# Bias strips read backwards from overlapping table rows, and x copied out of PSUM once

## The chip, the cores and the metric

The kernel runs on one core of a Trainium2 chip. The metric is the device time of one execution in microseconds (us). Three runs of the kernel before took 2470.0, 2471.08 and 2473.52 us; their median is 2471.08 us.

## The reference

Two layers of a decoder trunk over one sequence of 512 tokens with 1024 channels, all in float32. Each layer does the following.

```python
h = rms_norm(x, g)                       # per token: x * rsqrt(mean(x*x) + eps) * g
proj = h @ w_in                          # one projection, cut into q, k, v, gates of two mixers
y_ret = (silu(g_r) * retention(q_r, k_r, v_r)) @ w_o_ret
y_nsa = nsa(q_n, kv_n, gate_n, ..., rel_bias) @ w_o_nsa
x = x + (sigmoid(m_a) * y_ret + sigmoid(m_b) * y_nsa) @ w_out
x = x + swiglu(rms_norm(x, g_ffn))       # feed-forward with 2816 hidden channels
```

`nsa` has 16 heads and three branches per head: compressed keys (31 blocks), selected blocks and a window. With 512 tokens the selected blocks and the window are both plain causal attention. Every softmax adds a bias that depends on the head and on the distance between query and key alone: `rel_bias[bucket(q - k), head]`. Distances below 16 have a bucket each, longer ones share buckets by their logarithm, and all from 128 on share the last. Keys ahead of the query are masked.

## The kernel before

**Layout and precision.** Activations are kept transposed, eight tiles of 128 channels by 512 tokens. Every float32 operand of a product is split into a rounded part `hi` and a rest `lo`: ScalarE (ACT) writes `hi` with a copy, VectorE (DVE) writes `lo` as the difference (`split`, L78; `split_scaled`, L82, which also multiplies by a gain per channel). A product is then three matmuls, hi·hi, hi·lo and lo·hi (`mm3`, L119). Weights come through the SP queue in pieces of up to 1 MB into three buffers `wr` (`raw`, L86) and are split into tiles `wh` and `wl`, three of each (`cut`, L94).

**Order of the work.** The Python code names the order in which instructions are issued to a planner. The planner sorts the instructions of each engine when the kernel is built, by what it takes to be ready, and hands out the buffers of one tag one after the other in program order. On the chip each engine works through its own list in that order, and so do the queues of SP, ACT and POOL (GpSimd), which issue the DMAs. Most small tiles share the tag `u` with 37 buffers.

**The stretch before the first attention head.** `setup` (L133) loads x in eight tiles (SP), gains (SP), the identity and masks (POOL), and transposes the gains into `cols` (L163, L165). `setup_bias` (L187) makes the bias of every head against distance with a small one-hot product (L196) and writes it to a DRAM table `bv` of 16 rows with 640 entries: 384 entries of the far value, then 256 entries of near distances in falling order (L198 to L201). `near_strips` (L203) reads from `bv` one tile per pair of heads in which partition p holds the row from entry p on (L211, POOL queue). Such a tile has the tokens in the wrong order, so it is multiplied by an anti-diagonal matrix `anti` (L216), copied out (L218) and written to a second DRAM table `nr` (L220, ACT queue). The products stand where `nsa_kv` runs the generator to its end (L322).

`start_x` (L265) transposes x on TensorE (PE), tile k into one PSUM bank. From that bank ACT writes `hh` (the gain times x, rounded), DVE writes `hl` (the rest), and ACT copies x itself into `xt` (L281), which the ACT queue stores to DRAM (L282). DVE also sums the squares of x (L274). The norm's factor per token is not in `h`; it is applied after the projections. It is worked out by `norm_stats` (L244, POOL does the power, L253) and spread over a tile `rb` by `norm_bcast` (L255: DVE writes `rep`, PE transposes it at L262, ACT copies it out at L263).

`nsa_kv` (L294) projects compressed keys and values (bank `f`, weights `wc`), then two key tiles (bank `a`, weights `wk`). `compress` (L352) multiplies by `rb`, adds position vectors (L366, L377), splits, and runs a product over 16 rows (L391). Then come queries and values.

**The attention heads.** `nsa` (L657) runs 16 heads in a pipeline over 18 steps. Each head has a strip of 128 x 512 biases (`bias_strip`, L223: two loads, the far half from `bv`, broadcast, and the near half from `nr`; eight buffers). `nsa_scores` (L517) takes the last (i+1)·128 columns of it in one DVE instruction that subtracts, adds the bias and takes the minimum (L537), and `nsa_cmp` (L466) reads every sixteenth column (L489). Other projections fill PE between the heads. Behind the heads come the retention, the mixing and the feed-forward part, and the second layer goes the same way.

Of the kernel before, what the change touches and what calls it, by code (L numbers as in the profile page):

```python
# [8 lines left out]
F32 = mybir.dt.float32  # L9
F32R = mybir.dt.float32r  # L10
AF = mybir.ActivationFunctionType
ALU = mybir.AluOpType
AX = mybir.AxisListType

P = 128
T = 512
D = 1024
NT = T // P
KD = D // P
# [3 lines left out]
HN = 16  # L23
# [4 lines left out]
BIG = 3e38  # L28
# [3 lines left out]
class Builder:  # L32
# [47 lines left out]
        (eng or self.nc.vector).tensor_sub(lo, src, hi.bitcast(F32))  # L80

    def split_scaled(self, hi, lo, src, col):  # L82
        self.nc.scalar.activation(hi, src, AF.Copy, scale=col)  # L83
        self.nc.vector.scalar_tensor_tensor(lo, src, col, hi.bitcast(F32), ALU.mult, ALU.subtract)  # L84

    def raw(self, srcs, kt, n):  # L86
# [46 lines left out]
    def setup(self):  # L133
        nc, a = self.nc, self.a
        self.bv = self.dr.tile([HN, 640], F32, tag="bv", name="bv")
        self.nr = self.dr.tile([HN, P, 256], F32, tag="nr", name="nr")
        self.ident = self.const("ident", [P, P])
        nc.gpsimd.dma_start(self.ident, a["c_ident"])
        rows = self.u("rows", w=P)

        def load_rows():
            for l in range(DEPTH):
                nc.sync.dma_start(rows[l * 8 : l * 8 + 8], a["norm_mix_g"][l].rearrange("(k p) -> k p", p=P))
                nc.sync.dma_start(rows[16 + l * 8 : 24 + l * 8], a["norm_ffn_g"][l].rearrange("(k p) -> k p", p=P))
            nc.sync.dma_start(rows[32:40], a["norm_final_g"].rearrange("(k p) -> k p", p=P))
            nc.sync.dma_start(rows[40:72], a["cmp_pos_k"].rearrange("l (r q) d -> (l r) (q d)", q=2))
            nc.sync.dma_start(rows[72:104], a["cmp_pos_v"].rearrange("l (r q) d -> (l r) (q d)", q=2))

        self.xnat = []
        for hf in range(2):  # L150
            for t in range(NT):
                xt = self.u("xnat")
                nc.sync.dma_start(xt, a["x"][0, t * P : (t + 1) * P, hf * 512 : (hf + 1) * 512])
                self.xnat.append(xt)
            if hf == 0:
                load_rows()
        self.setup_bias()
        self.anti = self.sb.tile([P, P], F32, tag="u", name="anti")
        nc.gpsimd.dma_start(self.anti, a["c_anti"])
        self.strips = self.near_strips()  # L160
        next(self.strips)
        ps = self.tp()
        nc.tensor.transpose(ps[:, :104], rows[:104, :], self.ident[:104, :104])  # L163
        self.cols = self.const("cols", [P, 104])
        nc.vector.tensor_copy(self.cols, ps[:, :104])  # L165
        self.gmix = [self.cols[:, l * 8 : l * 8 + 8] for l in range(DEPTH)]
        self.gffn = [self.cols[:, 16 + l * 8 : 24 + l * 8] for l in range(DEPTH)]
        self.pos = {"k": [self.cols[:, 40 + l * 16 : 56 + l * 16] for l in range(DEPTH)],
                    "v": [self.cols[:, 72 + l * 16 : 88 + l * 16] for l in range(DEPTH)]}
        self.mhalf = self.const("mhalf", [P, NT])  # L170
        nc.vector.memset(self.mhalf, -0.5)
        self.ones = self.const("ones", [P, 1])
        nc.vector.memset(self.ones, 1.0)
        self.rb = self.const("rb", [P, T])
        self.rstd = self.const("rstd", [P, NT])
        self.hrstd = self.const("hrstd", [P, NT])
        self.kcz = [self.const(f"kcz{g}", [P, 224], F32R) for g in range(2)]
        for g in range(2):
            nc.vector.memset(self.kcz[g].bitcast(F32), 0.0)
        self.xs = self.dr.tile([KD, P, T], F32, tag="xs", name="xs")  # L180
        self.gs = self.dr.tile([2 * KD, P, T], F32, tag="gs", name="gs")
        self.gr = self.dr.tile([4 * NSPILL, P, T], F32, tag="gr", name="gr")
        self.ys = self.dr.tile([KD, P, T], F32, tag="ys", name="ys")
        self.cmask = self.const("cmask", [P, NT, 32])
        nc.gpsimd.dma_start(self.cmask, a["c_cmask"].rearrange("p (i n) -> p i n", n=32))

    def setup_bias(self):  # L187

        nc, a = self.nc, self.a
        tab = self.u("tab", w=HN)  # L190
        nc.scalar.dma_start(tab[:32], a["rel_bias"])
        nc.vector.memset(tab[32:33], NEG)
        ohv = self.u("ohv", w=256)
        nc.scalar.dma_start(ohv[:33], a["c_ohv"])
        ps = self.mm()
        nc.tensor.matmul(ps[:HN, :256], tab[:33], ohv[:33], start=True, stop=True)  # L196
        near, far = self.u("near", w=256), self.u("far", w=384)
        nc.scalar.activation(near[:HN], ps[:HN, :256], AF.Copy)  # L198
        nc.vector.tensor_copy(far[:HN], ps[:HN, 0:1].broadcast_to([HN, 384]))
        nc.gpsimd.dma_start(self.bv[:, :384], far[:HN])  # L200
        nc.gpsimd.dma_start(self.bv[:, 384:], near[:HN])  # L201

    def near_strips(self):  # L203


        nc = self.nc
        back = []
        for t in range(HN // 2):
            b = self.u("back").rearrange("p (b n) -> p b n", b=2)
            row = self.bv[t : t + 1, 256 : 512]  # L210
            nc.gpsimd.dma_start(b, bass.AP(row.tensor, row.offset, [[1, P], [8 * 640, 2], [1, 256]]))  # L211
            back.append(b)
        yield
        for t in range(HN // 2):
            ps = self.tp()
            nc.tensor.matmul(ps, self.anti, back[t].rearrange("p b n -> p (b n)"), start=True, stop=True)  # L216
            near = self.u("near").rearrange("p (b n) -> p b n", b=2)
            nc.scalar.activation(near, ps.rearrange("p (b n) -> p b n", b=2), AF.Copy)  # L218
            for b in range(2):
                nc.scalar.dma_start(self.nr[t + 8 * b], near[:, b])  # L220
            yield

    def bias_strip(self, h):  # L223

        t = self.sb.tile([P, T], F32, tag="strip", name=self.nm("strip"), bufs=NST)
        self.nc.sync.dma_start(t[:, :256], self.bv[h : h + 1, :256].broadcast_to([P, 256]))
        self.nc.sync.dma_start(t[:, 256:], self.nr[h])
        return t


    def make_h(self, src, col):
# [12 lines left out]
    def norm_stats(self, acc=None, ss=None):  # L244
        nc = self.nc
        if ss is None:
            ps = self.tp()
            for t in range(NT):
                nc.tensor.matmul(ps[:, t : t + 1], acc[:, t * P : (t + 1) * P], self.ones, start=True, stop=True)
            ss = ps[:, :NT]  # L250
        var = self.small("var", NT)
        nc.vector.tensor_scalar(var, ss, 1.0 / D, 1e-6, ALU.mult, ALU.add)
        nc.gpsimd.tensor_tensor(self.rstd, var, self.mhalf, ALU.pow)  # L253

    def norm_bcast(self):  # L255
        nc = self.nc
# [8 lines left out]
    def start_x(self):  # L265
# [3 lines left out]
        for k in range(KD):  # L269
# [6 lines left out]
            for t in range(NT):  # L276
                nc.tensor.transpose(ps[:, t * P : (t + 1) * P], self.xnat[4 * (k // 4) + t][:, (k % 4) * P : (k % 4 + 1) * P],
                                    self.ident)
            h.append(self.make_h(ps, self.gmix[0][:, k : k + 1]))
            xt = self.u("xt")  # L280
            nc.scalar.activation(xt, ps, AF.Copy)  # L281
            nc.scalar.dma_start(self.xs[k], xt)  # L282

        def stats():
            s2 = self.small("s2", NT)
# [8 lines left out]
    def nsa_kv(self, l, h, q0):  # L294
        nc, w = self.nc, self.a["w_in"][l]
        view = lambda c, n, k0=0, kt=KD: w[k0 * P : (k0 + kt) * P, c : c + n].rearrange("(k p) n -> p k n", p=P)
        wc = self.wcols(w, 0, KD, C_KV, 256)
        psc = [self.proj_t(wc, j, h, "f") for j in range(2)]
        wk = self.raw([(lambda v: v[:, :, :P], view(C_KV + 256, P)), (lambda v: v[:, :, P:], view(C_KV + 512, P))], KD, 256)
        self.stats()  # L300
# [18 lines left out]
            next(comp[kind])  # L319
        psk.append(self.proj_t([self.cut(wk[:, :, P:])], 0, h, "a"))  # L320
        keys(0)
        for _ in self.strips:  # L322
            pass
        next(comp["k"])
        for _ in range(2):
            for _ in range(9):
# [139 lines left out]
    def nsa_cmp(self, quad, qs, heads, pc):  # L466
# [16 lines left out]
        nc.gpsimd.memset(z, NEG)  # L483
        for i in range(NT):
            n = min(NCMP, 7 + 8 * i)
            x0 = 415 - P * i
            for s in range(4):
                bias = heads[4 * quad + s]["strip"][:, x0 : x0 + 16 * (n - 1) + 1 : 16]
                nc.vector.tensor_tensor(z4[:, i, s, :n], p4[:, i, s, :n], bias, ALU.add)  # L489
            yield  # L490
        z3 = z.rearrange("p (c n) -> p c n", n=32)
# [25 lines left out]
    def nsa_scores(self, st):  # L517
# [15 lines left out]
        def soft(br, i, src):  # L533
            w = (i + 1) * P
            p = pr[br][i]
            c = slice(br * NT + i, br * NT + i + 1)
            nc.vector.tensor_tensor_reduce(p, src, strip[:, T - w :], -1.0, BIG, ALU.add, ALU.min, nmx[:, c])  # L537
            nc.scalar.activation(p, p, AF.Exp, scale=-1.0, bias=nmx[:, c], accum_out=sm[:, c])  # L538

        for i in range(2):  # L540
# [466 lines left out]
def constants():  # L1007
# [14 lines left out]
    dec = np.where(e >= 0, gam[:, None, None] ** np.maximum(e, 0) / 16.0, 0.0).astype(f)  # L1022
    return {
        "c_ident": np.eye(P, dtype=f),
        "c_anti": np.ascontiguousarray(np.eye(P, dtype=f)[::-1]),
        "c_cos": np.ascontiguousarray(np.cos(ang).T.astype(f)),
        "c_sin": np.ascontiguousarray(np.sin(ang).T.astype(f)),
        "c_ohv": onehot(511 - np.arange(384, 640)),
        "c_cmask": cmask,
        "c_dec": dec,  # L1030
    }
# [28 lines left out]
```

## Time and profile before

| | |
|---|---|
| median of three runs | 2471.08 us |
| the profiled execution, its own time | 2472.11 us |
| its span, first to last instruction | 2470.1 us |
| PE busy | 2410.7 us, 98% |
| DVE busy | 1408.9 us, 57% |
| ACT busy | 1031.1 us, 42% |
| POOL busy | 252.9 us, 10% |
| mean granted TensorE clock | 0.996 |

The profile is of one execution. A line of the timeline has the start in us, the duration, the engine, the line of the code, the tile written and the tiles read, how many instructions were merged, and in brackets the idle time before it with what ended it. PE's matmuls overlap in their pipeline, so their cost on a busy PE is the distance from one start to the next and not the duration shown. The engines SPq, ACTq and POOLq stand for the queues that issue DMAs.

### The profile page before, as it was taken

How to read it: one execution, taken by the hardware profiler on the slowest of the kernel's cores; microseconds unless marked ns; L12 is line 12 of the kernel's file. 1: busy time of each engine (PE TensorE's matmuls, PEld its weight loads, DVE VectorE, ACT ScalarE, POOL GpSimd, SP SyncE). 2: the span in 40 equal slices, each digit the busy share in tenths (PEclk: the TensorE clock that was granted, in tenths of full speed). 3: DMA queues.
4: the chain of work that ended last, by engine and by line, in shares of the span. 5: the costliest groups of instructions: out<-in, count | busy, mean ns of one | idle time of the engine just before them, and what ended most of it. 6: DMA issues, size and time to landing. Idle time of an engine off the chain costs nothing.

```text
span 2470.1 us, 29520 instructions
## 1 busy us (share of the span) xinstructions
PE 2410.7 (98%) x11131; PEld 1956.7 (79%) x11131; DVE 1408.9 (57%) x2796; ACT 1031.1 (42%) x1871; POOL 252.9 (10%) x226
## 2 busy tenths in 40 slices
PE   6999999999999999999989999999999999999998
PEld 4887778788888778888878777878888878888887
DVE  5678887444655643333467888864545655433334
ACT  4666666233333432222346666642333333322223
POOL 2000000010111121010110000001100301101010
PEclk9999999999999999999999999999999999999999
DMA  7632223523334422323345332235223424223221
GB/s 222 190 94 77 73 86 78 175 80 100 107 99 145 145 94 85 103 87 101 114 139 146 90 82 69 73 90 171 89 91 105 158 96 147 92 85 98 90 94 60
DMA packets 242970, 266.74 MB, mean 108 GB/s; under 512 B 43187, under 2 KB 189788, under 8 KB 242828
## 3 DMA queue, kind: packets, MB, share of 16 engines
q1 hardware_dynamic: 225328, 236.93, 31.8%
q10 hardware_dynamic: 16700, 25.60, 2.9%
q0 software_dynamic: 800, 2.34, 0.3%
q8 instruction: 87, 1.43, 0.2%
q14 instruction: 55, 0.45, 0.1%
HBM read 237.53 MB, written 27.30 MB: 107 GB/s over the span
## 4 chain that ended last, share of the span: by engine, by line
PE 80%; DVE 4%; ACT 2%; issue 1%; DMA 1%; POOL 0%; POOLq 0%; ACTq 0%; DVEq 0%
PE f L122 10%; PE f L123 10%; PE f L124 10%; PE a L124 7%; PE a L123 7%; PE a L122 7%; PE o L123 7%; PE o L124 7%; PE o L122 7%; PE t L588 2%; PE o L581 1%; PE o L580 1%; DVE p L568 1%; DVE wl L80 1%; PE a L556 1%
## 5 line engine op out<-in xcount | busy, mean ns | idle before, releaser
L79 ACT ACTIVATE wh<-wr 128x1024 fp32r<-128x1024 f32 (+3 forms) x406 | 397.0, 980 | 971.3 <-PE f L123 236.2
L80 DVE TENSOR_TENSOR wl<-wr,wh 128x1024 fp32r<-128x1024 f32 (+3 forms) x406 | 462.2, 1142 | 219.6 <-ACT wh L79 213.9
L122 PE MATMUL f<-hh,wh 128*128 128x512 f32 x936 | 374.2, 400 | 4.4 <-ACT hh L83 4.2
L123 PE MATMUL f<-hl,wh 128*128 128x512 f32 x936 | 370.3, 396 | 4.0 <-DVE hl L84 4.0
L124 PE MATMUL f<-hh,wl 128*128 128x512 f32 x936 | 370.5, 397 | 0.1
L122 PEld LDWEIGHTS f<-hh,wh 128*128 128x128 f32 x936 | 176.6, 189 | 41.4 <-ACT hh L83 5.6
L124 PEld LDWEIGHTS f<-hh,wl 128*128 128x128 f32 x936 | 176.6, 189 | 41.0 <-DVE wl L80 1.2
L123 PEld LDWEIGHTS f<-hl,wh 128*128 128x128 f32 x936 | 176.7, 189 | 39.1 <-DVE hl L84 5.6
L538 ACT ACTIVATE p<-p,nmx 128x512 f32<-128x512 f32 (+3 forms) x256 | 142.3, 556 | 67.4 <-DVE nmx L537 65.4
L80 DVE TENSOR_TENSOR pt<-t,pt 128x512 fp32r<-128x512 f32 (+3 forms) x256 | 123.2, 484 | 56.5 <-ACT pt L79 55.0
L124 PE MATMUL a<-hh,wl 128*128 128x512 f32 x360 | 145.0, 403 | 9.7 <-DVE wl L80 9.7
L122 PE MATMUL a<-hh,wh 128*128 128x512 f32 x360 | 145.5, 404 | 0.0
L123 PE MATMUL a<-hl,wh 128*128 128x512 f32 x360 | 144.9, 402 | 0.0
L79 ACT ACTIVATE pt<-t 128x512 fp32r<-128x512 f32 (+3 forms) x256 | 109.4, 430 | 71.7 <-PE t L588 66.6
L891 POOL TENSOR_TENSOR fa<-fa,rb 128x512 f32<-128x512 f32 x44 | 77.2, 1755 | 570.0 <-ACT fa L890 570.0
L537 DVE CUSTOM_DVE_ANT_0 p<-a,strip 128x512 f32<-128x512 f32 (+3 forms) x256 | 119.4, 483 | 18.1 <-PE a L557 11.7
L122 PE MATMUL o<-hh,wh 128*128 128x512 f32 x304 | 120.1, 395 | 0.0
L124 PE MATMUL o<-hh,wl 128*128 128x512 f32 x304 | 120.0, 395 | 0.0
L123 PE MATMUL o<-hl,wh 128*128 128x512 f32 x304 | 119.9, 395 | 0.0
L588 PE MATMUL t<-ident,p 128*128 128x128 f32 x640 | 113.7, 273 | 0.0
L588 PEld LDWEIGHTS t<-ident,p 128*128 128x128 f32 x640 | 81.3, 141 | 24.3 <-issue 2.2
L580 PE MATMUL o<-pt,vs 128*128 128x512 f32 (+3 forms) x256 | 91.4, 360 | 1.4 <-ACT pt L79 1.3
(433 smaller groups left out, 4873.1 us busy)
## 6 DMA issues: line engine op xcount, KB each, us to landing
wr<-in_w_in SPq DMA_DIRECT2D x66, 1024.0 KB, 5.4
wr<-in_w_ffn_in SPq DMA_DIRECT2D x44, 1024.0 KB, 5.2
wr<-in_w_ffn_out SPq DMA_DIRECT2D x18, 1024.0 KB, 5.0
wr<-in_w_o_ret SPq DMA_DIRECT2D x16, 1024.0 KB, 5.1
wr<-in_w_in SPq DMA_DIRECT2D x36, 256.0 KB, 4.4
gs<-mt ACTq DMA_DIRECT2D x32, 256.0 KB, 2.0
wr<-in_w_o_nsa SPq DMA_DIRECT2D x16, 512.0 KB, 7.0
ga<-gs SPq DMA_DIRECT2D x32, 256.0 KB, 2.7
```

The source lines that it names most:

```text
L79: self.nc.scalar.activation(hi, src, AF.Copy)
L80: (eng or self.nc.vector).tensor_sub(lo, src, hi.bitcast(F32))
L122: self.nc.tensor.matmul(ps, lh, rh, start=start and i == 0, stop=False)
L123: self.nc.tensor.matmul(ps, lh, rl, start=False, stop=False)
L124: self.nc.tensor.matmul(ps, ll, rh, start=False, stop=stop and i == n - 1)
L537: nc.vector.tensor_tensor_reduce(p, src, strip[:, T - w :], -1.0, BIG, ALU.add, ALU.min, nmx[:, c])
L538: nc.scalar.activation(p, p, AF.Exp, scale=-1.0, bias=nmx[:, c], accum_out=sm[:, c])
L556: nc.tensor.matmul(ps[:, :w], qh[:, ts], ks[:, br, :w], start=True, stop=False)
L568: nc.vector.tensor_scalar(pr[br][i], pr[br][i], sm[:, c : c + 1], None, ALU.mult)
L580: nc.tensor.matmul(po[:, j * P :], lhs, th, start=br == 0 and j == 0, stop=False)
L588: nc.tensor.transpose(pt[:, (i - j) * P : (i - j + 1) * P], pr[br][i][:, j * P : (j + 1) * P], self.ident)
L891: nc.gpsimd.tensor_mul(t, t, self.rb)
```

## The change

- The table `bv` is turned round: 256 near entries first, for distances from -127 to 128, then 384 entries of the far value. The near part is copied out of PSUM by DVE in place of ACT.
- `near_strips` goes, with `anti`, the eight loads, the products, the copies and the table `nr`. A strip is now one load in which partition p holds the table's row from entry p on for 512 entries (2 KB per partition, each row shifted by one entry against the next). A strip so loaded has the distances rising from left to right, so L537 and L489 read it from right to left, with a step of -1 and of -16.
- In `start_x` ACT copies the PSUM bank into `xt` first, and both `hh` and `hl` are made from `xt`. The store of `xt` moves from the ACT queue to the POOL queue.
- In layer 0 ACT's splits of the first weights, `wc`, are ordered behind the `hh` of k = 2 (`issue_after` adds an order among the instructions of one engine, here ACT; `last_hi` hands that instruction out). `last_rstd` is set and not used in the lines shown.

```diff
     def setup_bias(self):
-        nc.scalar.activation(near[:HN], ps[:HN, :256], AF.Copy)
-        nc.vector.tensor_copy(far[:HN], ps[:HN, 0:1].broadcast_to([HN, 384]))
-        nc.gpsimd.dma_start(self.bv[:, :384], far[:HN])
-        nc.gpsimd.dma_start(self.bv[:, 384:], near[:HN])
+        nc.vector.tensor_copy(near[:HN], ps[:HN, :256])
+        nc.vector.tensor_copy(far[:HN], ps[:HN, 255:256].broadcast_to([HN, 384]))
+        nc.gpsimd.dma_start(self.bv[:, :256], near[:HN])
+        nc.gpsimd.dma_start(self.bv[:, 256:], far[:HN])
-    def near_strips(self):
...
     def bias_strip(self, h):
         t = self.sb.tile([P, T], F32, tag="strip", name=self.nm("strip"), bufs=NST)
-        self.nc.sync.dma_start(t[:, :256], self.bv[h : h + 1, :256].broadcast_to([P, 256]))
-        self.nc.sync.dma_start(t[:, 256:], self.nr[h])
+        row = self.bv[h : h + 1, :T]
+        self.nc.sync.dma_start(t, bass.AP(row.tensor, row.offset, [[1, P], [1, T]]))
         return t
+    def backwards(t, c, n, step=1):
+        v = t[:, c : c + 1]
+        return bass.AP(v.tensor, v.offset, [v.ap[0], [-step, n]])
...
     def start_x(self):
-            h.append(self.make_h(ps, self.gmix[0][:, k : k + 1]))
             xt = self.u("xt")
             nc.scalar.activation(xt, ps, AF.Copy)
-            nc.scalar.dma_start(self.xs[k], xt)
+            h.append(self.make_h(xt, self.gmix[0][:, k : k + 1]))
+            if k == 2:
+                self.first_h = self.last_hi
+            nc.gpsimd.dma_start(self.xs[k], xt)
...
     def nsa_kv(self, l, h, q0):
-        wc = self.wcols(w, 0, KD, C_KV, 256)
+        if l == 0:
+            with self.tc.issue_after(self.first_h.ins):
+                wc = self.wcols(w, 0, KD, C_KV, 256)
+        else:
+            wc = self.wcols(w, 0, KD, C_KV, 256)
...
-        for _ in self.strips:
-            pass
...
-                bias = heads[4 * quad + s]["strip"][:, x0 : x0 + 16 * (n - 1) + 1 : 16]
+                bias = self.backwards(heads[4 * quad + s]["strip"], 96 + P * i, n, 16)
...
-            nc.vector.tensor_tensor_reduce(p, src, strip[:, T - w :], -1.0, BIG, ALU.add, ALU.min, nmx[:, c])
+            nc.vector.tensor_tensor_reduce(p, src, self.backwards(strip, w - 1, w), -1.0, BIG, ALU.add, ALU.min, nmx[:, c])
```

## Rows read from the trace of the kernel before

**Rows 1.** Stages; columns: stretch, length, busy time per engine, clock, DMA share, GB/s.
```profile
17.00:50.00 33.00, 25.45 (x94) 17.90 (x94) 20.36 (x42) 16.30 (x24) 9.32 (x18) 1.00 0.80 259
50.00:60.00 10.00, 4.00 (x21) 3.32 (x21) 9.85 (x27) 4.89 (x10) 0.00 (x0) 0.88 0.48 81
60.00:75.00 15.00, 15.00 (x54) 10.37 (x53) 4.84 (x5) 6.60 (x11) 0.00 (x0) 0.85 0.93 292
100.00:450.00 350.00, 341.17 (x1755) 278.67 (x1755) 278.27 (x790) 224.69 (x539) 15.68 (x15) 1.00 0.32 88
```

The engines in these rows stand in the order PE, PEld (weight loads of PE), DVE, ACT, POOL.

**Rows 2.** Timeline of ACT, from the first weights on.
```profile
16.64 2.95 ACT L79 ACTIVATE wh<-wr 128x1024 fp32r<-128x1024 f32 x3 [1.21 <-DMA wr<-in_w_in]
19.50 0.67 ACT L83 ACTIVATE hh<-t,cols 128x512 fp32r<-128x512 f32 x1
24.37 0.60 ACT L281 ACTIVATE xt<-t 128x512 f32<-128x512 f32 x1 [4.21 <-DVE hl L84]
```

**Rows 3.** Waits from 20 to 50 us; columns: sum in us, times, longest.
```profile
ACT xt L281 <- DVE hl L84: 10.2, 7, 4.2
```

**Rows 4.** Timeline of DVE.
```profile
17.73 3.50 DVE L80 TENSOR_TENSOR wl<-wr,wh 128x1024 fp32r<-128x1024 f32 x3 [1.72 <-ACT wh L79]
21.14 0.68 DVE L274 CUSTOM_DVE_ANT_0 junk<-xnat 128x512 f32<-128x512 f32 x1
40.83 0.42 DVE L258 COPY rep<-rstd 128x512 f32<-128x512 f32 x1
```

**Rows 5.** Timeline of PE.
```profile
8.70 1.92 PE L277 MATMUL t<-ident,xnat 128*128 128x128 f32 x8
13.99 1.03 PE L196 MATMUL f<-ohv,tab 33*16 33x256 f32 x2
20.22 0.79 PE L122 MATMUL f<-hh,wh 128*128 128x512 f32 x1 [4.15 <-ACT hh L83]
44.77 1.05 PE L262 MATMUL t<-ident,rep 128*128 128x128 f32 x8
58.55 0.80 PE L124 MATMUL a<-hh,wl 128*128 128x512 f32 x1 [4.80 <-DVE wl L80]
59.14 0.63 PE L122 MATMUL a<-hh,wh 128*128 128x512 f32 x1
59.57 0.63 PE L123 MATMUL a<-hl,wh 128*128 128x512 f32 x1
66.44 2.83 PE L216 MATMUL t<-back,anti 128*128 128x512 f32 x6
68.71 0.68 PE L391 MATMUL o<-wl,p 128*128 128x256 f32 x1
74.20 0.39 PE L122 MATMUL f<-hh,wh 128*128 128x512 f32 x1
74.43 0.39 PE L123 MATMUL f<-hl,wh 128*128 128x512 f32 x1
```

**Rows 6.** Groups of instructions by form; columns as in the page's part 5.
```profile
L84 DVE SCALAR_TENSOR_TENSOR hl<-t,cols,hh 128x512 fp32r<-128x512 f32 x4 | 3.0, 748 | 3.5 <-ACT hh L83 3.5
L537 DVE CUSTOM_DVE_ANT_0 p<-a,strip 128x512 f32<-128x512 f32 x64 | 43.8, 685 | 8.0 <-PE a L557 7.3
L489 DVE TENSOR_TENSOR cz<-t,strip 128x31 f32<-128x31 f32 x32 | 4.5, 197 | 0.0
L489 DVE TENSOR_TENSOR cz<-t,strip 128x7 f32<-128x7 f32 x32 | 3.1, 157 | 5.6 <-PE t L478 5.5
```

**Rows 7.** Instructions by tile: count, duration ns min/median/max, first and last start us.
```profile
L84 DVE SCALAR_TENSOR_TENSOR hl<-strip,cols,hh x24: 743/746/1874, 841.1 to 2090.6; 128x512 fp32r<-128x512 f32 x24
L537 DVE CUSTOM_DVE_ANT_0 p<-a,strip x256: 269/483/695, 107.3 to 1625.1; 128x384 f32<-128x384 f32 x64, 128x128 f32<-128x128 f32 x32, 128x256 f32<-128x256 f32 x32
```

**Rows 8.** The line that loads `back`: its issue on POOL, and the time to landing.
```profile
L211 POOL DMA_DIRECT2D back<-bv x8: 704/716/753, 22.7 to 27.6; - x8
DMA to landing us min/median/max: 5.8/6.9/8.7
```

More of the change, by code (lines that the diff above doesn't have):

```diff
@@ L82, in split_scaled @@
     def split_scaled(self, hi, lo, src, col):
-        self.nc.scalar.activation(hi, src, AF.Copy, scale=col)
+        self.last_hi = self.nc.scalar.activation(hi, src, AF.Copy, scale=col)
         self.nc.vector.scalar_tensor_tensor(lo, src, col, hi.bitcast(F32), ALU.mult, ALU.subtract)
@@ L135, in setup @@
         self.bv = self.dr.tile([HN, 640], F32, tag="bv", name="bv")
-        self.nr = self.dr.tile([HN, P, 256], F32, tag="nr", name="nr")
         self.ident = self.const("ident", [P, P])
@@ L157, in setup @@
         self.setup_bias()
[L158 to L161, printed above, removed]
         ps = self.tp()
@@ L197, in setup_bias @@
         near, far = self.u("near", w=256), self.u("far", w=384)
-        nc.scalar.activation(near[:HN], ps[:HN, :256], AF.Copy)
-        nc.vector.tensor_copy(far[:HN], ps[:HN, 0:1].broadcast_to([HN, 384]))
-        nc.gpsimd.dma_start(self.bv[:, :384], far[:HN])
-        nc.gpsimd.dma_start(self.bv[:, 384:], near[:HN])
-    def near_strips(self):
[L206 to L221, printed above, removed]
+        nc.vector.tensor_copy(near[:HN], ps[:HN, :256])
+        nc.vector.tensor_copy(far[:HN], ps[:HN, 255:256].broadcast_to([HN, 384]))
+        nc.gpsimd.dma_start(self.bv[:, :256], near[:HN])
+        nc.gpsimd.dma_start(self.bv[:, 256:], far[:HN])
     def bias_strip(self, h):
         t = self.sb.tile([P, T], F32, tag="strip", name=self.nm("strip"), bufs=NST)
-        self.nc.sync.dma_start(t[:, :256], self.bv[h : h + 1, :256].broadcast_to([P, 256]))
-        self.nc.sync.dma_start(t[:, 256:], self.nr[h])
-        return t
+        row = self.bv[h : h + 1, :T]
+        self.nc.sync.dma_start(t, bass.AP(row.tensor, row.offset, [[1, P], [1, T]]))
+        return t
+    @staticmethod
+    def backwards(t, c, n, step=1):
+        v = t[:, c : c + 1]
+        return bass.AP(v.tensor, v.offset, [v.ap[0], [-step, n]])
     def make_h(self, src, col):
@@ L252, in norm_stats @@
         nc.vector.tensor_scalar(var, ss, 1.0 / D, 1e-6, ALU.mult, ALU.add)
-        nc.gpsimd.tensor_tensor(self.rstd, var, self.mhalf, ALU.pow)
+        self.last_rstd = nc.gpsimd.tensor_tensor(self.rstd, var, self.mhalf, ALU.pow)
     def norm_bcast(self):
@@ L485, in nsa_cmp @@
             n = min(NCMP, 7 + 8 * i)
-            x0 = 415 - P * i
             for s in range(4):
-                bias = heads[4 * quad + s]["strip"][:, x0 : x0 + 16 * (n - 1) + 1 : 16]
+                bias = self.backwards(heads[4 * quad + s]["strip"], 96 + P * i, n, 16)
                 nc.vector.tensor_tensor(z4[:, i, s, :n], p4[:, i, s, :n], bias, ALU.add)
@@ L1024, in constants @@
         "c_ident": np.eye(P, dtype=f),
-        "c_anti": np.ascontiguousarray(np.eye(P, dtype=f)[::-1]),
         "c_cos": np.ascontiguousarray(np.cos(ang).T.astype(f)),
         "c_sin": np.ascontiguousarray(np.sin(ang).T.astype(f)),
-        "c_ohv": onehot(511 - np.arange(384, 640)),
+        "c_ohv": onehot(np.arange(256) - 127),
         "c_cmask": cmask,
```

## The prediction

> **What bounds the kernel now.** I read the page's first part first: PE is busy for 98% of the span, so a change counts only where PE waits, where it does work that can go, or where it runs slowly. The table of stages then says where that is: PE stands for 7.5 us between 17 and 50 us, for 6.0 between 50 and 60, and is full from 60 to 75 [rows 1]. The first projection starts at 20.22 [rows 5]. The change works in these stretches and in the attention heads (100 to 450 us, and the same again in the second layer), where PE is idle for 8.8 of 350 us and DVE is busy for 278 [rows 1].
>
> The timelines of ACT and DVE show why PE starts late. PE has transposed the tiles of k = 0 and 2 by 10.6 [rows 5], but ACT's list has three splits of weights in front of the first `hh`, and the weights land at 16.64; `hh` follows at 19.50 [rows 2]. DVE has three `wl` (3.50 us) and four squares of x in front of the first `hl` [rows 4], and ACT's copy `xt` waits for that `hl` until 24.37 [rows 2]. ACT stands 10.2 us in seven such waits [rows 3]: the copy out of the bank comes behind DVE's read of the same bank, tile after tile. So `rep`, the end of the norm's chain on DVE, comes at 40.83 [rows 4], PE spreads it at 44.77 [rows 5], and compression can start. From there DVE is the bound: 9.85 of 10 us from 50 to 60 [rows 1], with PE waiting 4.80 us for a `wl` until 58.55 [rows 5]. [...]
>
> **The change part by part.** All sums are against the profiled execution, 2472.11 us (span 2470.1, 2.0 around it); it stands 1.0 above the median of the three runs.
>
> *The start.* With the order behind `hh` of k = 2 and no wait for DVE, ACT can work from 10.6 on: three tiles at 0.60 for `xt` [rows 2] and 0.67 for `hh` [rows 2] are 3.8 us, done by 14.4, before the weights land. The first `wh` ends about 17.6 (a third of 2.95 after 16.64 [rows 2]), and PE starts near 17.7 instead of 20.22. From there three engines could set when the norm is spread. ACT: three splits (2.95) and the five tiles left (5 x 1.27 = 6.4) end at 26.0. DVE: it can start at 15.0, when the bias product ends [rows 5], because the two table copies now stand on its list. I take 1.2 for both (the squares over 512 columns take 0.68 each [rows 4]; bounds 0 and 1.4); eight squares at 0.62 (21.14 to 23.62, four of them [rows 2, 4]) are 5.0; eight `hl` at 0.75 [rows 6] 6.0; three `wl` 3.5; `rep` 0.4; 0.5 for small ones. Sum 16.6, end 31.6. PE: two projections of 24 matmuls stand before the spreading. If the first 6 us run at 0.43 a matmul (14 of them) and 34 at 0.23, that is 13.8 us; with 2 us of transposes left over, 33.5. PE is the last of the three: 33.5 against 44.77, 11 us earlier. If every step also waits once for the one before (1.3 a tile over the five late tiles, 6.5 us), 5 us are left; if the two spread over less work, 13 at most, since PE cannot start before 17.6. I take 11, nearest to the sums.
>
> *The stretch behind.* Compression and second keys give DVE the same work as before, so its full stretch moves forward whole: 0. If the late `wl` now finds room in front of `z`, the 4.80 us wait goes as well and with it the slow 5.7 us behind (13 matmuls at 0.20 more each, 2.6): 0 to -7.4. I take 0, because the order on DVE's list is the planner's and nothing in the edit touches it.
>
> *The exchange products.* Sixteen PE instructions at L216; six take 66.44 to 68.71, 0.38 each [rows 5], so 6.1 us in all. Four come in front of a wait and are worth nothing; the other twelve lie where PE is busy 15.0 of 15 us [rows 1]: 12 x 0.38 = 4.5. If PE then only meets DVE earlier, 0. I take 4. The eight copies and sixteen stores that go from ACT lie where ACT has 6.6 of 15 us of work [rows 1] and nobody waits for it: 0.
>
> *The stores of x on POOL's queue.* Eight issues at 0.72 (the price of the `back` loads there [rows 8]) replace eight of those loads on POOL, which is 9.3 of 33 us busy [rows 1]. Queued behind them on POOL is the power of the norm; with the last `xt` near 25 (half a tile before ACT's end) it still runs by 28, before `rep` is due. But they now leave early, three of them (0.75 MB) beside the first weights; at the 259 GB/s of that stretch [rows 1] that is 0 to 2.9 us for the first `wh`. Since the stores and the `back` loads that go (2 MB) pull opposite ways, I take 1.
>
> *Strips.* One load of 256 KB in place of two. The nearest row are the `back` loads, also 256 KB of overlapping rows, with 5.8 to 8.7 us to landing [rows 8]. The first reader is at 107.3 [rows 7], and L537 waits for PE alone [rows 6], so 0; without that cover it would be 8.7 once per layer.
>
> *Reading backwards.* 256 instructions at L537, on average 320 columns, and 128 short ones at L489. Forward, L537 costs at most (695 - 269)/384 = 1.11 ns per column [rows 7]; L489, with a step of 16 forward, (197 - 157)/24 = 1.67 [rows 6]. A backward step is in no row. Lower end 0, since reading in the other order moves no column less; upper end the step-16 slope, 0.56 x 320 x 256 = 46 us of DVE. I take 0: a step of -1 is nearest to a step of 1. [...]
>
> *x read from SBUF.* `hl` takes 748 ns from PSUM [rows 6] and 746 from SBUF [rows 7], so 0. [...]
>
> Sum: -11 + 0 - 4 + 1 + 0 = **-14 us**, 2458.1 for the profiled execution and 2457 for the median.
>
> **The rivals.**
>
> *A, more goes:* the wait at 58.55 goes too. For it: DVE is idle for 12.6 of 33 us before 50 [rows 1], so there is room. Against: the order of its list. -14 - 7.4, so 2450.
>
> *B, ACT waits again:* the edit orders only the splits of `wc`; the split of `wk` was the third of the three [rows 2] and may stay in front of `hh`. It began at 18.6, so ACT would give three tiles by 23.5 and `wh` by 24.5; PE starts 4.3 us later than before, not 2.5 earlier, and the change does not do what it says. ACT still loses its 10.2 us of waits. Of the 11 about 4 are left: 2464; with the full 2.9 us of stores, 2466.
>
> *C, the gain is given back:* the planner sorts the whole program anew. PE idles 17.6 us over the heads of two layers; if that grows by half to all of it, 9 to 14 us come back: 2466 to 2471.
>
> *D, slower:* the backward reads cost DVE time in the heads. Place: L537, whose result ACT and then PE wait for. At the step-16 slope 46 us; DVE has 72 us of 350 free per layer [rows 1], but in pieces. With half exposed 2457 + 23 = 2480, with all 2503. It decides from 14 us / 256 = 55 ns exposed per read; from there the change is no gain.
>
> **How the numbers follow.** Forecast 0.58 (its own range 2452 to 2462), A 0.09, B 0.16, C 0.10, D 0.07. What this kernel's measurement can tell from no change is 0.2%, 4.9 us: faster means below 2466.1. That is the forecast and A, two thirds of B and a third of C: 0.80. Same: the rest of B and most of C and a little of D, 0.13. Slower: 0.07. The range leaves out half of A below 2448 and, above 2469, D and a part of C.
>
> **What would show it.** Right, step by step: `hh` of k = 0 in front of every `wh`, near 11 us; first projection at 17 to 19; no `xt` waiting for `hl`; spreading at L262 near 33; no L216; L537 at 483 ns in the median and its first start near 93 instead of 107.3, its last near 1611. Wrong: a `wh` in front of `hh` (B); L537 slower than 500 ns (D); a first L537 that is 14 us early and a last one that is not (C). The forecast as a whole fails if the first L537 is less than 7 us early.

## The result, and the profile after

The kernel after takes 2455.45 us in the median (2454.37 to 2456.08, 4 runs), the kernel before 2472.3 beside it (4 runs): 16.85 us less, a ratio of 0.9933 with an interval of 0.9922 to 0.9945. 2457.0 was predicted. The profiled execution took 2455.72 us (span 2453.9).

Stages of the kernel after, columns as in [rows 1]:

```profile
17.00:50.00 33.00, 25.62 (x101) 19.68 (x102) 26.85 (x61) 16.91 (x27) 6.76 (x15) 0.96 0.77 239
50.00:60.00 10.00, 10.00 (x43) 7.96 (x43) 6.54 (x8) 5.22 (x7) 0.00 (x0) 0.80 0.66 210
60.00:75.00 15.00, 15.00 (x84) 12.82 (x83) 10.91 (x16) 10.57 (x17) 0.00 (x0) 1.00 0.51 147
...
100.00:450.00 350.00, 341.10 (x1725) 277.04 (x1724) 270.68 (x759) 215.20 (x505) 15.92 (x15) 1.00 0.32 89
```

Up to 107 us all has moved. In the last row PE is as busy as in [rows 1]; the window is fixed in time and the heads start 17 us earlier in it, so the other columns do not hold the same work. Timeline of ACT after, against [rows 2]:

```profile
9.71 0.60 ACT L262 ACTIVATE xt<-t 128x512 f32<-128x512 f32 x1
10.34 0.72 ACT L83 ACTIVATE hh<-xt,cols 128x512 fp32r<-128x512 f32 x1
...
12.82 0.72 ACT L83 ACTIVATE hh<-xt,cols 128x512 fp32r<-128x512 f32 x1
16.17 1.06 ACT L79 ACTIVATE wh<-wr 128x1024 fp32r<-128x1024 f32 x1 [2.63 <-DMA wr<-in_w_in]
...
31.81 1.06 ACT L79 ACTIVATE wh<-wr 128x1024 fp32r<-128x1024 f32 x1 [6.63 <-PE f L123]
```

Timeline of DVE after, against the last of [rows 4]:

```profile
32.90 1.22 DVE L80 TENSOR_TENSOR wl<-wr,wh 128x1024 fp32r<-128x1024 f32 x1 [4.05 <-ACT wh L79]
34.04 0.42 DVE L240 COPY rep<-rstd 128x512 f32<-128x512 f32 x1
```

Timeline of PE after, against [rows 5]; L244 is the spreading, L262 before:

```profile
17.28 0.79 PE L122 MATMUL f<-hh,wh 128*128 128x512 f32 x1 [0.47 <-ACT wh L79]
20.60 0.80 PE L124 MATMUL f<-hh,wl 128*128 128x512 f32 x1 [1.67 <-DVE wl L80]
...
35.79 1.05 PE L244 MATMUL t<-ident,rep 128*128 128x128 f32 x8
...
49.17 0.79 PE L124 MATMUL a<-hh,wl 128*128 128x512 f32 x1 [4.86 <-DVE wl L80]
49.77 0.63 PE L122 MATMUL a<-hh,wh 128*128 128x512 f32 x1
50.19 0.63 PE L123 MATMUL a<-hl,wh 128*128 128x512 f32 x1
...
54.03 0.40 PE L123 MATMUL a<-hl,wh 128*128 128x512 f32 x1
54.26 0.39 PE L124 MATMUL a<-hh,wl 128*128 128x512 f32 x1
```

The reads of the strips, by line (L522 was L537, L474 was L489):

```profile
L522 DVE CUSTOM_DVE_ANT_0 p<-a,strip x256: 269/484/694, 90.5 to 1608.2; 128x384 f32<-128x384 f32 x64, 128x128 f32<-128x128 f32 x32, 128x256 f32<-128x256 f32 x32
```

```profile
L474 DVE TENSOR_TENSOR cz<-t,strip x128: 152/176/204, 111.8 to 1551.1; 128x7 f32<-128x7 f32 x32, 128x15 f32<-128x15 f32 x32, 128x23 f32<-128x23 f32 x32, 128x31 f32<-128x31 f32 x32
```

Three distances tell where the time went. The spreading comes at 35.79 instead of 44.77 (-9.0). The wait for the late `wl`, 4.86 us against 4.80, is still there and ends at 49.17 instead of 58.55 (-9.4). The first head starts at 90.5 instead of 107.3 [rows 7] (-16.8), so another 7.4 went between that wait and the heads. The last head is 16.9 early: from the first head to the last, nothing changed.

### The profile page after: what moved, and what is told of

It reads as the page before. It is cut to its first block, busy times and chain, and to the rows that moved or that the text cites. A ratio compares the mean times of both kernels' runs of the same rounds, so it can differ in the third digit from the quotient of the medians.

```text
span 2453.9 us, 29372 instructions
## 1 busy us (share of the span) xinstructions
PE 2404.7 (98%) x11115; PEld 1956.1 (80%) x11115; DVE 1409.4 (57%) x2797; ACT 1025.3 (42%) x1862; POOL 252.2 (10%) x225
## 4 chain that ended last, share of the span: by engine, by line
PE 89%; DVE 6%; ACT 3%; issue 1%; POOL 1%; DMA 0%; SPq 0%; POOLq 0%; ACTq 0%; DVEq 0%
PE f L123 12%; PE f L122 12%; PE f L124 12%; PE a L124 8%; PE a L123 7%; PE a L122 7%; PE o L124 7%; PE o L122 7%; PE o L123 7%; PE t L573 2%; DVE p L553 1%; PE o L566 1%; PE o L565 1%; PE a L541 1%; PE a L542 1%
## 5 line engine op out<-in xcount | busy, mean ns | idle before, releaser
L522 DVE CUSTOM_DVE_ANT_0 p<-a,strip 128x512 f32<-128x512 f32 (+3 forms) x256 | 119.5, 484 | 18.1 <-PE a L542 11.5
```

The costliest lines, as they stand in the source:

```text
L522: nc.vector.tensor_tensor_reduce(p, src, self.backwards(strip, w - 1, w), -1.0, BIG, ALU.add, ALU.min, nmx[:, c])
```

## Experiments

Of each kernel the first and last start of L522 (whatever its line number there) are given as "heads": the first measures the start of the first layer, the distance between them what came later. That distance is 1517.8 us before and 1517.7 after. One profile each, so differences of a microsecond mean little. The kernels ran in several rounds, each beside the kernel before, whose median lay between 2471.1 and 2472.3 us; two kernels of different rounds compare to about 1 us. The edits are shortened to what differs.

**Each part alone.** strips_only is the kernel after with the old order in `start_x` (and no `issue_after`); x_only is the kernel before with the new one (and the `issue_after`).

```
# strips_only, start_x              # x_only: the reverse edit of before
- xt = copy(ps); h = make_h(xt)     - h = make_h(ps); xt = copy(ps)
- nc.gpsimd.dma_start(xs, xt)       - nc.scalar.dma_start(xs, xt)
+ h = make_h(ps); xt = copy(ps)     + xt = copy(ps); h = make_h(xt)
+ nc.scalar.dma_start(xs, xt)       + nc.gpsimd.dma_start(xs, xt)
```

> The changed kernel with start_x as it was before (h made from the PSUM bank, xt copied last, stored from ACT's queue) and no order on the splits of wc: the strips alone. Theory (two gains that add: the start and the strips): the products (4.5 to 6 us of PE) and the short waits of PE behind them go, and a part of the start, since the loads of back no longer hold the buffers in front of hh; 6 to 9 us below the kernel before, about 2465, first head near 100. Rival (the exchange was all that mattered, the start is a by-product): 14 us or more below, about 2457.

> The kernel before with the new start_x (xt copied first, h made from it, stored from POOL's queue) and with the order behind hh of k = 2, but with the exchange product kept. Theory: the start alone, 9 to 11 us below the kernel before, about 2462; spreading of the norm near 36, DVE's full stretch moved forward whole, the products still on PE behind it. Rival: 0 to 4 us below, since the products' loads come late on POOL's queue and hold the rest back.

strips_only: 2462.19 us against 2472.28 (ratio 0.996, 0.9946 to 0.9973), heads 95.3 to 1613.0. x_only: 2471.94 (0.9998, 0.9989 to 1.0007), nothing, heads 107.9 to 1625.8. The parts give 10.1 and 0.3 alone and 16.9 together: strips_only lies between its theory and its rival, x_only where its rival had it. That fells the reading on which my sum stood, a gain of the start made by the `x` edit and one of the products made by the other. PE of strips_only:

```profile
40.55 1.05 PE L244 MATMUL t<-ident,rep 128*128 128x128 f32 x8
...
54.31 0.79 PE L124 MATMUL a<-hh,wl 128*128 128x512 f32 x1 [4.80 <-DVE wl L80]
```

The strips part alone moves the spreading by 4.2 us: the table's copy has left ACT, and the first `hh` comes at 17.21, behind one split of weights and not three (which of the two counts was not tried apart). From the wait's end to the first head it gives 7.8 (54.31 to 95.3, against 58.55 to 107.3), as the kernel after does (7.4). The `x` part then adds 5.1 at the wait (54.31 to 49.17). Why nothing in x_only? Its POOL and DVE:

```profile
22.97 5.69 POOL L211 DMA_DIRECT2D back<-bv  x8 [5.14 <-DMA bv<-far]
28.65 1.14 POOL L284 DMA_DIRECT2D xs<-xt  x2
```

```profile
36.57 0.75 DVE L84 SCALAR_TENSOR_TENSOR hl<-xt,cols,hh 128x512 fp32r<-128x512 f32 x1 [7.44 <-DMA xs<-xt]
```

The stores of `x` queue on POOL behind eight `back` loads that wait for the bias table; the tiles come free late, and DVE stands 7.44 us for one.

**Is it POOL's queue?** x_only_act stores from ACT's queue again; x_free has both table copies on DVE, as after, and issues `anti` and the `back` loads behind the stores.

```
# x_only_act: x_only with           # x_free: x_only with
- nc.gpsimd.dma_start(xs, xt)       - activation(near, ps); anti, back loads in setup
+ nc.scalar.dma_start(xs, xt)       + vector.tensor_copy(near, ps); both behind start_x
```

> The x part alone (as in x_only), with one thing changed: the stores of x leave from ACT's queue, as before the change, and no longer stand on POOL's queue behind the wait for the bias table and the eight back loads. Theory (POOL's queue held the stores, so the tiles xt came free late and DVE's and PE's waits of 7.44 and 6.02 us near 36 took the gain of the start): these two waits go, the last hh is done near 26, the norm is spread near 40 and not at 46.8, and the time falls to 2460-2465. Rival (ACT's copy of the table until 15.6 and DVE's list hold the start whichever queue stores): within 3 us of x_only, 2468-2473.

> The x part alone once more, with the exchange products, their loads and stores all kept, but freed of the bias chain: both copies of the bias table are DVE's (as in after), and the eight back loads and the load of anti are issued behind the stores of x on POOL's queue instead of ahead of them. In x_only and x_only_act the first store of x was issued at 28.65 and 24.40, behind transfers that wait for the bias table, and ACT's copy of the table ran until 14.5 in front of hh. Theory (what took the start's gain was this order, not the products): first projection 17-18.5, no wait for hl of several us, norm spread 35.5-38, first head 97-99, time 2462-2465. Rival (the start's gain needs the exchange gone, since its tiles and transfers fill the same stretch): 2468-2472.

x_only_act: 2470.75 against 2471.07 (0.9997, 0.9988 to 1.0006), heads 105.8 to 1625.5. The theory missed: the first store now waits on ACT's queue, and ACT with it.

```profile
24.40 0.36 ACTq L284 DMA_DIRECT2D xs<-xt  x1
24.81 0.60 ACT L280 ACTIVATE xt<-o 128x512 f32<-128x512 f32 x1 [9.06 <-DMA strip<-bv]
```

By the profile it waits for a strip load, which reads the table, as the `back` loads do (here those start at 21.70, after 5.30 us for the table's store). Nothing in the code ties the two, and no trace shows what does. So this kernel did not test POOL's queue alone. x_free takes the stores off both waits (with three edits at once). x_free: 2469.91 against 2471.61 (0.9995, 0.9987 to 1.0004), heads 105.2 to 1622.4. The time is the rival's; of the theory only the start held. DVE and PE of x_free:

```profile
40.70 1.23 DVE L80 TENSOR_TENSOR wl<-wr,wh 128x1024 fp32r<-128x1024 f32 x1 [3.20 <-ACT wh L79]
41.84 0.42 DVE L254 COPY rep<-rstd 128x512 f32<-128x512 f32 x1
```

```profile
17.24 0.80 PE L122 MATMUL f<-hh,wh 128*128 128x512 f32 x1 [0.46 <-ACT wh L79]
...
43.47 1.05 PE L258 MATMUL t<-ident,rep 128*128 128x128 f32 x8
...
73.21 0.39 PE L124 MATMUL f<-hh,wl 128*128 128x512 f32 x1
76.51 0.38 PE L393 MATMUL o<-wh,pt 128*128 128x256 f32 x1 [2.91 <-ACT wh L79]
```

The start is that of the kernel after (17.24 against 17.28). But the planner put three `wl` of later weights in front of `rep` on DVE's list, each with a wait for its `wh` (9.3 us in all), and matmuls of the keys in front of the spreading on PE's. The lead is not lost by that: PE starts the last matmul of the first projection of the queries at 73.21, and the kernel before, after the same matmuls, at 78.85, so 5.6 us of lead are left. At 76.51 PE then waits for a split that ACT gives late. ACT of x_free, and then of the kernel before:

```profile
70.56 1.08 ACT L214 ACTIVATE near<-t 128x512 f32<-128x512 f32 x2 [4.47 <-DMA nr<-near]
71.18 3.71 ACTq L216 DMA_DIRECT2D nr<-near  x4
75.40 1.06 ACT L79 ACTIVATE wh<-wr 128x1024 fp32r<-128x1024 f32 x1
```

```profile
76.85 0.60 ACT L218 ACTIVATE near<-t 128x512 f32<-128x512 f32 x1 [4.09 <-DMA nr<-near]
...
78.66 1.04 ACT L79 ACTIVATE wh<-wr 128x1024 fp32r<-128x1024 f32 x1
```

In both, ACT's exchange copies stand over 4 us for the stores to `nr`, and the next split of weights comes behind them; PE of before waits for it twice:

```profile
78.85 0.40 PE L124 MATMUL f<-hh,wl 128*128 128x512 f32 x1
79.75 0.39 PE L391 MATMUL o<-wh,pt 128*128 128x256 f32 x1 [0.51 <-ACT wh L79]
81.01 0.39 PE L391 MATMUL o<-wl,pt 128*128 128x256 f32 x1 [0.87 <-DVE wl L80]
```

PE of x_free goes on 3.2 us ahead of before (76.51 against 79.75) where it had been 5.6 ahead, and its first head is 2.1 ahead. My new theory: with the exchange in place, ACT's copies and stores set when PE goes on near 77 to 80, and most of what is gained earlier is lost there.

**The same gate, from another side.** wk_early is the kernel after with the late `wl`'s split moved up, in both layers; before_wk_early is the kernel before with the same edit.

```
  psk = [self.proj_t([self.cut(wk[:, :, :P])], 0, h, "a")]
+ wk1 = self.cut(wk[:, :, P:])
...
- psk.append(self.proj_t([self.cut(wk[:, :, P:])], 0, h, "a"))
+ psk.append(self.proj_t([wk1], 0, h, "a"))
```

> The kernel after, with the split of the second half of wk moved in the program to right behind the first projection of the keys, ahead of the compression's tiles, so that its subtraction stands earlier on DVE's list (in both layers with this code). It tests what the wait of 4.86 us for that wl before 49.17 is worth. Theory: the wait goes and the slow matmuls behind it (0.43 us apart until 54) with it; the first head starts at 84-86 instead of 90.5, and the time is 2447-2451. Rival (the wait only moves: with 1.2 us more in front of them rep and the compression's subtractions are late, and PE stands for these): first head 89-91, 2454-2457.

> The kernel before with one edit that the change doesn't make: the split of the second half of wk stands right behind the first projection of the keys in the program (as in wk_early). Theory (the wait of 4.8 us for that wl before 58.55, and the slower matmuls behind it, are worth the same before and after the change): 6 to 9 us faster than before, 2462-2465, in two layers together. Rival (in before DVE is later at this point, so the wait only goes elsewhere): 2467-2472.

wk_early: 2447.94 us against 2471.07 (0.9903, 0.989 to 0.9917), 7.5 below the kernel after (6.3 if each is compared with the kernel before of its own round), the fastest kernel of the study and, in time, within its theory's range. before_wk_early: 2471.67 against 2471.61 (1.0002, 0.9992 to 1.0011), nothing, as its rival had it. In wk_early the wait of 4.86 is gone (the next are 1.57, at 48.96, and 0.96, at 51.13); heads 86.8 to 1600.3, so 3.7 us in the first layer and 4.2 behind. (Its profiled run lies 1.7 under its median.) The slow matmuls stayed, though the theory had them go with the wait: the one at 51.72 takes 0.43 us to the next, and the granted clock is 0.83 from 50 to 60, against 0.80 after. before_wk_early also loses its wait of 4.80, and then stands elsewhere. Its ACT and PE:

```profile
73.57 1.08 ACT L218 ACTIVATE near<-t 128x512 f32<-128x512 f32 x2 [5.26 <-DMA nr<-near]
```

```profile
73.64 0.40 PE L124 MATMUL f<-hh,wl 128*128 128x512 f32 x1
78.46 0.58 PE L392 MATMUL o<-wh,pt 128*128 128x256 f32 x1 [4.42 <-ACT wh L79]
```

It comes to the end of the first projection of the queries 5.2 us ahead of before (73.64 against 78.85), and goes on only 1.3 ahead (78.46 against 79.75). Its heads are 108.6 to 1622.8: nothing gained in the first layer, where the exchange is, and by the profile 3.6 us in the second, where there is none. (The profiled run lies 1.7 under the median, and the median shows no gain, so the 3.6 is the less sure of the two.) This supports my new theory. What holds the stores themselves, the transfers (DMA 0.93 busy there [rows 1], 0.51 after) or whatever held the store in x_only_act, no run tells, and a kernel with the stores on another queue was not tried.

**What the exchange costs.** products_back is the kernel after with eight products and their copies, nothing loaded or stored; exchange_back has sixteen stores from ACT's queue as well, in the first layer only. The results are not used.

```
  keys(0)
+ for t in range(HN // 2):
+     matmul(ps, self.ident, self.rb); activation(near, ps, Copy)
+     # exchange_back alone, both only if l == 0:
+     for b in range(2): nc.scalar.dma_start(nr[t + 8 * b], near[:, b])
```

> The kernel after, with eight products of 128x512 (ident times the spread norm, both resident) and their eight copies by ACT put where the exchange products stood; nothing is loaded, stored or read of them. It prices the products by themselves; the results go nowhere. Between the end of the wait for wl and the first attention head the change saved 7.4 us. Theory (all of it is the products: twelve of sixteen instructions, 0.59 us each with their weight loads and the slower clock around them): 2462-2464, first head near 97.5 instead of 90.5. Rival (0.38 us each as read from the group of six, the rest came from elsewhere, the back loads, the stores to nr or the clock): 2458-2460.5, first head 93.5-95. Second rival (PE only meets its later wait earlier): 2455-2456.5.

> The kernel after, with eight products, their eight copies by ACT and sixteen stores from ACT's queue to a table that nobody reads, in the first layer alone, where the exchange stood. products_back had its eight products in both layers (an oversight), so its 8.2 us are two layers; its first head was at 95.0, 4.5 later than after. Theory (the products are 4.5 of the 7.4 us, the rest is ACT held by the stores: its wait of 4.09 us at 76.85 in before and PE's waits of 0.51 and 0.87 behind it): first head 96.5-98, time 2461.5-2463.5. Rival (the stores and copies are free, the rest came from elsewhere): first head 94.5-95.5, time 2459.5-2460.5.

products_back: 2463.61 against 2471.07 (0.9971, 0.996 to 0.9982); exchange_back: 2461.53 against 2471.61 (0.9962, 0.9949 to 0.9974). The time of products_back lies in its theory's range only because its products stand in both layers; its first head is the first rival's. exchange_back came as its theory had it. Their heads, and PE of products_back:

```profile
L526 DVE CUSTOM_DVE_ANT_0 p<-a,strip x256: 268/484/693, 95.0 to 1618.1; 128x384 f32<-128x384 f32 x64, 128x128 f32<-128x128 f32 x32, 128x256 f32<-128x256 f32 x32
```

```profile
L531 DVE CUSTOM_DVE_ANT_0 p<-a,strip x256: 268/482/692, 96.9 to 1614.7; 128x384 f32<-128x384 f32 x64, 128x128 f32<-128x128 f32 x32, 128x256 f32<-128x256 f32 x32
```

```profile
49.31 0.79 PE L124 MATMUL a<-hh,wl 128*128 128x512 f32 x1 [4.01 <-DVE wl L80]
...
55.94 5.50 PE L312 MATMUL t<-rb,ident 128*128 128x512 f32 x12
```

The first head goes from 90.5 to 95.0 by the products (4.5 us; four of the sixteen instructions stand in front of the wait and shorten it, twelve behind cost what they take), and to 96.9 with the stores (1.9 more, from one profile each). ACT of exchange_back stands for its stores too, 1.55 us before 63.29 and 1.33 before 66.08, less than the 4.09 of before. In the second layer of products_back its eight products add 5.4 between the first and the last head. Of the 7.4 us, 1.0 is not reproduced; the loads of the strips from `nr` and `bv`, which exchange_back leaves out, are an untested candidate.

**The other terms.** no_order drops the `issue_after`; forward reads the strips left to right, so that the biases are those of other distances; store_on_act stores `x` from ACT's queue; wk_sq is wk_early with four sums of squares on ACT.

```
# no_order                          # forward
- with issue_after(first_h):        - self.backwards(strip, w - 1, w)
      wc = self.wcols(...)          + strip[:, T - w :]     (L474: its step-16 form)
# store_on_act                      # wk_sq, four of the eight
- nc.gpsimd.dma_start(xs, xt)       - vector.tensor_tensor_reduce(junk, xn, xn)
+ nc.scalar.dma_start(xs, xt)       + first_h = activation(junk, xn, Square, accum_out)
```

> The changed kernel without the order on ACT's splits of wc. On ACT's list a wh then stands in front of xt of k = 0 and waits for the weights (16.2). Theory: ACT's work on the first three tiles (3.8 us) moves behind that wait; h of k = 7 comes 4 us later, PE starts 2 us later and loses 2 to 4 us against the changed kernel, about 2458.5. Rival (PE is paced by its slow first 6 us and by DVE anyway, so the order is worth nothing): within 1 us of the changed kernel, 2455 to 2456.

> The changed kernel with the strips read from left to right, as the kernel before did, so that the biases stand in the wrong places. Theory: a backward step costs nothing; within 1.5 us of the changed kernel, the reads of the strips at 484 ns in the median in both, those of every sixteenth column at 176. Rival: a part of the 46 us of DVE time that the step-16 slope would give is paid: 5 us or more below the changed kernel, and the reads shorter by 30 ns or more.

> The kernel after, with the eight stores of x put back on ACT's queue. Theory (POOL has nothing else to do at the start once the back loads are gone, and ACT has: eight issues of about 0.33 us stand before its splits): 0 to 3 us slower than after, 2455.5-2458.5, hh k=7 done 1 to 3 us later. Rival (the last stores leave POOL only at 28.4 and hold tiles or rstd): 1 to 3 us faster, 2452.5-2454.5.

> wk_early, with the first four of the eight sums of squares of x moved from DVE to ACT, into its idle time between the third hh (13.5) and the first wh (16.2). Theory (until the norm is spread DVE's list of work ends last, and it is 2.5 us shorter): the norm is spread 1 to 2.5 us earlier and the time is 2445.5-2447. Rival (ACT starts its splits later by what the squares take past 16.2, and DVE waits for it): 2447.5-2451.

no_order: 2457.27 against 2472.28 (0.9943, 0.9931 to 0.9956), heads 93.2 to 1611.1; its ACT starts so:

```profile
16.61 1.06 ACT L79 ACTIVATE wh<-wr 128x1024 fp32r<-128x1024 f32 x1 [7.22 <-DMA wr<-in_w_in]
...
19.00 0.71 ACT L83 ACTIVATE hh<-xt,cols 128x512 fp32r<-128x512 f32 x1
```

The time is between the theory's loss and the rival's. The order moves the first `hh` by 8.7 us (19.00 to 10.34) and the wait's end by 2.4 (51.55 to 49.17): most of the idle time that it fills cost little. forward: 2454.59 against 2472.28 (0.993, 0.9918 to 0.9943), L522 at 269/484/693 and L474 at 151/175/203: here a backward step costs nothing (269/484/694 and 152/176/204 in the kernel after). store_on_act: 2458.6 against 2471.07 (0.9947, 0.9935 to 0.996), heads 93.2 to 1611.2, 3.2 us slower, a little more than the theory had, and by another way than the issues: ACT stands behind a store, and the first projection starts at 21.19 instead of 17.28.

```profile
19.22 0.33 ACTq L266 DMA_DIRECT2D xs<-xt  x1
19.59 0.60 ACT L262 ACTIVATE xt<-a 128x512 f32<-128x512 f32 x1 [5.16 <-DMA wr<-in_w_in]
```

wk_sq: 2448.26 against 2471.61 (0.9909, 0.9895 to 0.9922), no better than wk_early; the theory missed. DVE has its last `hl` of the start done at 27.4 instead of 28.9, but `rep` comes at 34.62 (33.64 in wk_early), behind a `wl` that waits for ACT's `wh`.

## Why the prediction came out right

The time was right within 1.6 us, and of the steps that the text named as its test these came so: the first `hh` at 10.34, the first projection at 17.28, no `xt` waiting for `hl`, no L216, L537's reads at 484 ns. The spreading, forecast near 33, came at 35.79, and the first head, forecast near 93, at 90.5. Two terms were mis-sized in opposite directions, and the sum hid part of it: the saving was 16.85 us and not 14, and the time looks nearer than that because the kernel before ran 1.2 us slower beside the new one than in the forecast's three runs.

*The start, -11, measured -9.0 to -9.4.* I had DVE's sum of work, with `rep` as its last term, end at 31.6 and PE's at 33.5; `rep` came at 34.04 and the spreading at 35.79. DVE was not busy for longer than I counted, but a fourth `wl` (1.22), of the compression weights, stood in front of `rep`, and DVE stood 4.05 us for its `wh`, as ACT had stood 6.63 for it until PE had read an older one. I summed each engine by itself and left out that tiles are handed round. PE did not wait for `rep`: from 20.60 to the spreading its matmuls follow one another without a gap. The 0.43 and 0.23 us a matmul of PE's sum are distances in [rows 5], from 59.14 to 59.57 and from 74.20 to 74.43. Against that sum PE lost 2.5 us on its first two matmuls (17.28 to 20.60, with a wait of 1.67 for a `wl`) and 1.6 on seven matmuls of the keys that were sorted in front of the spreading, and the 2 us of transposes were over before. The reason I gave was also only half of it. I put the start on the freed ACT; strips_only has 4.2 of it without the `x` edit, the order is worth 2.4, and without the strips part the `x` edit is worth nothing.

*The exchange, -4, measured -7.4.* The products' own 4.5 was right as far as one profile tells (products_back). Wrong is the step "the eight copies and sixteen stores that go from ACT lie where ACT has 6.6 of 15 us of work and nobody waits for it: 0". The share says little: most of ACT's idle time in that stage was for PE (3.59 us before 66.41, 2.5 for L216's results). But from 72.76 ACT stood 4.09 us for its own stores, nearly half of it behind the stage's end, and PE waited for what came after, 0.51 and 0.87 us. With stores the first head comes 1.9 later. And that place was a gate: as long as it stood, of a lead of 5.6 us in front of it 3.2 were left behind it (x_free), and of 5.2 only 1.3, with none at the first head (before_wk_early).

*The stretch behind, 0.* Right: the wait stayed (4.86). Rival A's price of 7.4 for it, 4.80 and 13 matmuls at the 0.20 us between the two distances of [rows 5], was twice too high: wk_early removes it and gains 3.7 in that layer, since smaller waits and slow matmuls behind it take over.

*Stores of x, +1.* The first `wh` starts at 16.17 instead of 16.64, so no loss shows. The stores do not leave early, as I had it, but from 15.78 on, behind the table's two, when the first weights are nearly in. They are cheaper to issue than the `back` loads that I took as their price: 0.56 against 0.72 each, by the first of POOL's groups here.

```profile
15.78 1.67 POOL L266 DMA_DIRECT2D xs<-xt  x3
...
28.39 1.16 POOL L266 DMA_DIRECT2D xs<-xt  x2
```

*Strips, backward reads, x from SBUF: 0 each.* Right. The strips land within 8.6 us and nobody waits. Forward and backward agree to 1 ns, for a step of 1 (484 and 484) and of 16 (175 and 176). `hl` takes 738 ns from SBUF against 748 from PSUM [rows 6], a gap of 10 ns in the mean of the group, of the size by which SBUF reads differ among themselves (746 in [rows 7]):

```profile
L84 DVE SCALAR_TENSOR_TENSOR hl<-xt,cols,hh 128x512 fp32r<-128x512 f32 x8 | 5.6, 738 | 0.0
```

*The rivals.* A did not come: the wait stayed. B did not come: all three splits stand behind the third `hh`, and even without the order (no_order) the loss is 1.8 us and not 7. C did not come: the last head is as early as the first. (In x_free the planner sorted the spreading back to 43.47, but that is ahead of the heads, and a lead of 5.6 us was left behind it.) D is ruled out by forward.

## What to carry to other kernels

Two edits on one critical path need not add: price each one also with the other left out, and look for the stage behind it that would become the gate. An engine with a low busy share in a full stretch may be standing for its own stores, there or just behind it (ACT, busy for 6.6 of 15 us, stood 4.09 for them from 72.76); look at what ended its idle time before calling it room. Moving the split of a late weight up in the program paid 6 to 7.5 us here, and nothing that could be measured while the exchange stood behind it.

## What the hardware showed that I had not expected

A store on ACT's queue can hold ACT's next instruction, by the profile for a load on SP's queue that the code does not tie to it: 9.06 us in x_only_act for a strip load, 5.16 in store_on_act for a load of weights. Why is not shown. Issuing a plain store of 256 KB from POOL took 0.54 to 0.61 us in the kernel after, an overlapping load in two runs per partition 0.72 [rows 8], a store from ACT 0.33 to 0.36 in store_on_act. The granted clock fell again at the wait that ends at 49.17, as it had at the one that ends at 58.55 (0.87 from 55 to 58.55 before, 0.50 from there to 64): PE had stood since 44.3, the clock was 0.82 in the mean from 44 to 49, 0.50 from 49 to 54 and 1.00 from 54 to 75 (matmuls 0.43 us apart at 49.77, 0.23 at 54.03). The clock in the rows does not show all slow matmuls: from 20.60 to 26.31 they stand 0.43 us apart as well, and the clock given for that stretch is 1.00.
